# A two-layer hybrid decoder step on eight cores: unnormalised MLP input, conv and pool first, column chunks of w_in, time-major sample state

## The chip, the cores and the metric

The kernel runs on the eight cores of one Trainium2 chip. Each core takes one prompt sequence and four sample sequences; the cores exchange nothing. The metric is the device time in microseconds (us) of the slowest core. A program on eight cores has a second, slower state, in which the cores of one die show a lower granted TensorE clock; all comparisons below use runs of the fast state. Engines: PE multiplies matrices, DVE, ACT and POOL are the vector, scalar and general engines, SP only issues DMAs here. POOL and ACT can issue DMAs too.

## The reference, cut to what matters

```python
for layer in range(2):
    h = rmsnorm(x, norm1_g); proj = h @ w_in              # 1024 -> 2560
    u, q, k, v, gb, gc, gh = split(proj)
    y_pool = pool_mix(u)                                  # causal windows 2/4/8/16, 256 channels
    q, k = rope(rmsnorm(q)), rope(rmsnorm(k))
    y_attn = merge(dilated_attention(q, k, v))            # 3 groups: (128,1) (512,4) (2048,16)
    y_conv = gb * conv3(gc * gh)                          # 384 channels
    x = x + concat(y_pool, y_attn, y_conv) @ w_out        # 768 -> 1024
    x = x + square(relu(rmsnorm(x, norm2_g) @ w_up)) @ w_down   # 1024 -> 4096 -> 1024
# outputs also: the new sample caches, cache[:, 8:] followed by 8 new rows, for both layers
```

On each core x is 2080 tokens (32 sample, 2048 prompt), held as 5 blocks of 416 columns, with the 1024 channels as 8 chunks of 128 partitions. Moving the old cache rows into the output is a plain copy in HBM. Per layer and core it is four sequences times three caches of 120, 504 and 2040 KB (of 1024 bytes), 10.9 million bytes.

## The kernel before

The program is written as many small coroutines ("procs"). A planner in Python simulates the engines, decides from estimated costs and priorities in which order each engine gets its instructions, and derives the semaphore waits from reads and writes of named regions.

```python
def copy_caches(l, n, after):                 # HBM -> HBM, touches no buffer of SBUF
    yield wait(after)                         # planner event only
    for g in range(3):
        W = WINS[g]
        yield ops(ld(lambda e: e.dma_start(out=o_kv_s[g][l, n, 0:W - 8, :], in_=caches[g][l, n, 8:W, :]), 2000 * W, slot=("c2c", g)))
# ... placed after: att(l,0), att(l,1), and two points in the MLP

def reload(l, b, after):                      # x again, for the residual, into a slot that was scratch
    yield wait(*after)
    for h in range(2):
        yield ops(ld(...X[:, s, 4*h:4*h+4, :] <- xin or xpark...))     # ld = SP's queue
        for c in range(4 * h, 4 * h + 4):
            K.fire(ev("xres", l, b, c))

def norm(l, which, b, X, ..., on_pe=False):
    # sum of squares: on PE (layer 0's first norm, and one block of layer 1's) or by adds on POOL (all others)
    # rst = exp(-0.5 * ln(mean + eps)) on ACT
    # HT[c] = X[c] * g[c] * rst on DVE, 8 instructions, bf16: the input of w_in or w_up

def down(l, fb, b, oc):                       # MLP, quarter fb of the 4096
    # 8 matmuls, then X[oc] += psum on DVE
```

In the slots of x live, during a layer's front, the scratch of conv, pool, QKV and attention. So x is parked and loaded again ("reload") once a slot's scratch is dead, and out_proj's residual add (DVE, `X = psum + X`) waits for it.

## Time and profile before

| | before |
|---|---|
| time, median of 3 (range) | 1606.16 us (1603.94 to 1606.86) |
| PE, DVE, ACT, POOL busy, slowest core | 1424, 857, 479, 347 us of 1607 |
| layer 0 front / MLP / layer 1 front / MLP | 375 / 453 / 309 / 470 us |

The table of windows of the kernel before shows four stretches: per engine the busy time and (x) the instructions, then the granted PE clock, the DMA engines' busy share and GB/s.

```profile
core 7: us, PE busy (x) PEld busy (x) DVE busy (x) ACT busy (x) POOL busy (x), PEclk, DMA share, GB/s
0.00:375.00 375.00, 273.58 (x1755) 156.16 (x1756) 224.07 (x434) 151.22 (x362) 140.70 (x186) 0.90 0.67 126
375.00:828.00 453.00, 451.01 (x2563) 250.81 (x2562) 219.12 (x368) 110.50 (x217) 59.93 (x63) 1.00 0.30 61
828.00:1137.00 309.00, 240.64 (x1705) 140.92 (x1704) 202.24 (x398) 124.75 (x309) 123.77 (x154) 0.92 0.55 110
1137.00:1607.00 470.00, 459.02 (x2589) 253.92 (x2586) 211.99 (x349) 92.08 (x180) 23.01 (x24) 0.99 0.24 52
```

The two MLP stretches are PE work at full clock. The fronts have gaps, a lower clock, and DMA that is busy more than half the time. Who waited for whom on PE in the first 400 us of before (engine and line, what it waited for, total, times, longest):

```profile
PE psum L864 <- ACT sqr L863: 37.8, 16, 9.8
...
PE psum L1402 <- DVE big L1406: 9.9, 3, 5.7
```

L864 sums the squares of the norm on PE: those waits are mostly for x to arrive (ACT's squares, L863, waited 26.8 us for x in the first 120 us). L1402 is out_proj, held by the residual add L1406, which waits for the reload. Timeline of SP: start, duration, what; merged:

```profile
124.35 0.80 SPq L1462 DMA_DIRECT2D kv_s<-c  x1
...
288.55 0.58 SPq L916 DMA_DIRECT2D big<-xin  x1
...
315.58 11.48 SPq L916 DMA_DIRECT2D big<-xin  x8
327.11 3.65 SPq L1462 DMA_DIRECT2D kv_s<-c  x6
```

L916 is the reload, L1462 the cache copies. Two sequences' copies go out between 124 and 218 us; the other two go at 327 us.

### The profile page before, as it was taken

The page shows a single profiled execution, that of the slowest core. Times are in us where ns is not written, and L with a number is a line of the kernel's source. Part 1 is how long each engine was busy: PE and PEld are TensorE (multiplying, and loading weights), DVE is VectorE, ACT ScalarE, POOL GpSimd, SP SyncE. Part 2 cuts the span into 40 slices and gives each one's busy share as a digit, 9 for nine tenths or more (in the row PEclk, how much of TensorE's full clock was granted, in tenths as well). Part 3 has the DMA queues.
Part 4 walks back from the last instruction along what each step waited for, and adds up shares of the span by engine and source line. Part 5 has one row for each costly group of instructions (what it writes and reads, how often), then busy time and mean ns, then how long its engine had stood idle before and what let it go on. Part 6 is the DMA issues. An engine that isn't in the chain of part 4 may idle for free.

```text
span 1607.4 us, 26919 instructions; the slowest of 8 cores (1582.2 to 1607.4 us)
## 1 busy us (share of the span) xinstructions
PE 1424.3 (89%) x8606; PEld 801.8 (50%) x8606; DVE 857.4 (53%) x1547; ACT 478.5 (30%) x1065; POOL 347.4 (22%) x426
## 2 busy tenths in 40 slices
PE   2778788779999999999977789868699999999998
PEld 1344455434555555555544455534355555555554
DVE  1667667467444444445676666746854444444443
ACT  2544345424112212113433444532412111211211
POOL 2344344344000000012434344323500000000000
PEclk9789889899999999999999999989899999999999
DMA  8758541999223023033264452189920601400112
GB/s 184 167 75 71 111 111 34 137 234 171 49 49 58 1 53 53 1 63 76 86 148 57 68 133 74 36 127 241 169 50 1 105 1 28 79 1 1 44 69 102
DMA packets 67897, 133.32 MB, mean 83 GB/s; under 512 B 25832, under 2 KB 35112, under 8 KB 67376
## 3 DMA queue, kind: packets, MB, share of 16 engines
q0 software_dynamic: 27648, 54.14, 23.2%
q1 hardware_dynamic: 40112, 77.47, 18.1%
q8 instruction: 72, 1.18, 0.3%
q14 instruction: 65, 0.53, 0.2%
HBM read 159.71 MB, written 47.89 MB: 129 GB/s over the span
## 4 chain that ended last, share of the span: by engine, by line
PE 69%; DMA 10%; DVE 8%; issue 5%; POOL 4%; ACT 3%; SPq 1%; DVEq 0%; ACTq 0%; POOLq 0%
PE psum L1441 28%; PE psum L1425 27%; PE psum L923 5%; PE psum L1071 4%; DMA vspill<-big 4%; DMA big<-xin 3%; PE psum L1402 3%; DVE big L889 3%; DMA big<-w_in 2%; POOL sqr L875 1%; POOL big L1110 1%; POOL big L956 1%; DVE big L1118 1%; DVE big L1117 1%; DMA kv_p<-big 1%
## 5 line engine op out<-in xcount | busy, mean ns | idle before, releaser
L1425 PE MATMUL psum<-big 128*128 128x416 bf16 x2560 | 464.3, 341 | 4.3 <-DVE big L1406 2.2
L1441 PE MATMUL psum<-big 128*128 128x416 bf16 x2560 | 461.0, 339 | 1.5 <-DVE big L1431 1.5
L1430 ACT ACTIVATE big<-psum 128x416 f32<-128x416 f32 x320 | 165.1, 517 | 650.8 <-PE psum L1425 426.4
L1425 PEld LDWEIGHTS psum<-big 128*128 128x128 bf16 x2560 | 251.0, 98 | 206.8 <-issue 9.6
L1441 PEld LDWEIGHTS psum<-big 128*128 128x128 bf16 x2560 | 250.0, 98 | 201.5 <-issue 3.0
L1431 DVE TENSOR_TENSOR big<-psum,big 128x416 bf16<-128x416 f32 x320 | 187.9, 591 | 284.5 <-ACT big L1430 274.0
L1444 DVE TENSOR_TENSOR big<-psum,big 128x416 f32<-128x416 f32 x320 | 188.5, 591 | 200.4 <-PE psum L1441 199.7
L923 PE MATMUL psum<-big 128*128 128x416 bf16 x880 | 179.3, 355 | 10.6 <-ACT big L984 5.6
L1071 PE MATMUL psum<-big 128*128 128x384 bf16 (+1 forms) x816 | 156.5, 350 | 10.0 <-ACT big L1260 3.0
L889 DVE SCALAR_TENSOR_TENSOR big<-big 128x416 bf16<-128x416 f32 x160 | 120.7, 823 | 49.7 <-ACT big L886 42.6
L875 POOL TENSOR_TENSOR sqr<-sqr,big 128x416 fp32r<-128x416 f32 x98 | 107.9, 1101 | 172.1 <-ACT big L874 161.9
L923 PEld LDWEIGHTS psum<-big 128*128 128x128 bf16 x880 | 87.3, 102 | 80.5 <-issue 25.3
L1071 PEld LDWEIGHTS psum<-big 128*128 128x128 bf16 (+1 forms) x816 | 82.5, 104 | 73.9 <-issue 31.4
L1402 PE MATMUL psum<-big 128*128 128x416 bf16 x480 | 94.4, 356 | 15.4 <-DVE big L1406 13.2
L1110 POOL TENSOR_TENSOR big<-big 128x512 f32<-128x512 f32 (+1 forms) x54 | 66.7, 1238 | 184.2 <-DVE big L1104 170.2
L844 POOL DMA_DIRECT2D big<-w_up x16 | 12.2, 767 | 334.3 <-PE psum L1425 333.8
L874 ACT ACTIVATE big<-big 128x416 f32<-128x416 f32 x98 | 52.7, 547 | 98.4 <-DVE big L1406 62.5
L1402 PEld LDWEIGHTS psum<-big 128*128 128x128 bf16 x480 | 47.9, 102 | 58.3 <-issue 25.6
L956 POOL TENSOR_TENSOR big<-big 128x430 f32<-128x430 f32 (+7 forms) x72 | 64.7, 903 | 36.3 <-ACT big L952 28.4
L1406 DVE TENSOR_TENSOR big<-psum,big 128x416 f32<-128x416 f32 x80 | 45.3, 587 | 45.5 <-PE psum L1402 25.5
L864 PE MATMUL psum<-sqr,onesr 128*128 128x416 f32 x48 | 24.5, 567 | 40.3 <-ACT sqr L863 37.8
L1117 DVE TENSOR_TENSOR big<-big 128x128 f32<-128x128 f32 (+1 forms) x108 | 42.4, 393 | 27.7 <-POOL big L1110 21.8
(98 smaller groups left out, 892.9 us busy)
## 6 DMA issues: line engine op xcount, KB each, us to landing
big<-xin SPq DMA_DIRECT2D x20, 832.0 KB, 12.1
big<-w_up POOLq DMA_DIRECT2D x16, 1024.0 KB, 15.4
big<-w_down POOLq DMA_DIRECT2D x16, 1024.0 KB, 13.3
kv_s<-c SPq DMA_DIRECT2D x8, 2040.0 KB, 40.2
big<-w_in POOLq DMA_DIRECT2D x16, 576.0 KB, 8.7
xpark<-big SPq DMA_DIRECT2D x10, 832.0 KB, 3.6
big<-xpark SPq DMA_DIRECT2D x10, 832.0 KB, 15.7
yout<-big SPq DMA_DIRECT2D x20, 416.0 KB, 2.4
```

The costliest lines, as they stand in the source:

```text
L875: K.spawn(freeing(pool(BL, lambda e, i=i: e.tensor_tensor(out=acc, in0=acc.bitcast(F32), in1=SS[i], op=ALU.add), [ka, ("ss", i)], [ka]), P ...
L889: yield ops(*[dve(BL + 100, lambda e, c=c: e.scalar_tensor_tensor(out=HT[:, c, BL * b:BL * b + BL], in0=X[:, si, c, :], scalar=NG[:, l, wh ...
L923: yield ops(pe([(BL, lambda e, d=d: e.matmul(bank(bi)[:, 0:BL], lhsT=WA[:, d, col0:col0 + 128], rhs=HT[:, d, BL * b:BL * b + BL], start=(d ...
L956: return pool(n, lambda e: e.tensor_tensor(out=out, in0=a, in1=b_, op=ALU.add), r, w)
L1071: yield ops(pe([(384, lambda e, d=d, j=j, jj=jj: e.matmul(pq[0:R, jj, 0:384].rearrange("p (k n) -> p k n", k=3), lhsT=lhs(d, j), rhs=wg[:, ...
L1110: yield ops(pool(256 * J, lambda e: e.tensor_tensor(out=qf[0:R, 0:J, 0:256], in0=qf[0:R, 0:J, 0:256], in1=GQK[0:R].unsqueeze(1).to_broadca ...
L1402: yield ops(pe([(BL, lambda e, c=c: e.matmul(bank(bi)[:, 0:BL], lhsT=WO[c // 2][:, c % 2, 128 * oc:128 * oc + 128], rhs=mix(c, b), start=( ...
L1425: yield ops(pe([(BL, lambda e, d=d: e.matmul(bank(bi)[:, 0:BL], lhsT=WU[i][:, d, 128 * fc:128 * fc + 128], rhs=HT[:, d, BL * b:BL * b + BL ...
L1430: yield ops(act(BL, lambda e: e.activation(out=RL[ri], in_=bank(bi)[:, 0:BL], func=AF.Relu), [("ps", bi)], [("rl", ri)]))
L1431: yield ops(dve(BL, lambda e: e.tensor_tensor(out=AT[a][:, fc, :], in0=bank(bi)[:, 0:BL], in1=RL[ri], op=ALU.mult), [("ps", bi), ("rl", ri ...
L1441: yield ops(pe([(BL, lambda e, f=f: e.matmul(bank(bi)[:, 0:BL], lhsT=WD[i][:, f, 128 * oc:128 * oc + 128], rhs=AT[a][:, f, :], start=(f == ...
L1444: yield ops(dve(BL, lambda e: e.tensor_tensor(out=X[:, s, oc, :], in0=bank(bi)[:, 0:BL], in1=X[:, s, oc, :], op=ALU.add), [("ps", bi), ("x ...
```

## The change

In six parts:

1. The MLP takes x*g unnormalised. With v = mean(x^2) + eps, the squared ReLU makes the MLP's output scale by 1/v. So x is multiplied by v before the MLP's sums are added and the whole by 1/v at the end. Up-projections wait no longer for the norm.
2. Conv and pool get better priorities than attention.
3. w_in comes in column chunks (conv's c, h, b; pool; then q, k, v), x and weights in one order on POOL's queue.
4. The sample state is time-major: one transfer per kind instead of one per chunk.
5. Sums of squares are all on POOL (none on PE). The x reload goes from SP's queue to POOL's, the V spill from SP's to ACT's.
6. Cache copies are placed at four points in the MLP. Priorities and costs in the planner are retuned.

The core of the diff:

```diff
-    def norm(l, which, b, X, s, si, src, out_ev, before=(), on_pe=False):
+    def sumsq(l, which, b, X, s, si, src):          # POOL adds only, one buffer
...
+    def cast2(l, b, c):
+        yield wait(ev("xm", l, b, c))
+        yield ops(act(BL, ... out=HT[:, c, ...], in_=X[:, s, c, :], func=AF.Copy, scale=NG[:, l, 1, c:c + 1]))
+    def norm2(l, b):
+        bi = yield from sumsq(l, 1, b, ...)
+        yield ops(act(BL, ... out=VB[b], in_=bank(bi)[:, 0:BL], func=AF.Identity, scale=1.0 / D, bias=EPSC))
+        for c in range(8):
+            yield ops(dve(BL + 60, ... X[:, s, c, :] = X[:, s, c, :] * VB[b]))
+        yield ops(dve(BL + 60, ... e.reciprocal(out=VB[b], in_=VB[b])))
...
-    def reload(l, b, after):
-            yield ops(ld(lambda e: e.dma_start(out=X[:, s, 4 * h:4 * h + 4, :], in_=src[...
+    def reload(l, b, h, after):
+        yield ops(ldc(lambda e: e.dma_start(out=X[:, s, 4 * h:4 * h + 4, :], in_=src[...      # ldc = POOL's queue
...
     def down(l, fb, b, oc):
+        if fb == 0:
+            yield wait(ev("xv", l, b, oc))
         yield ops(dve(BL, ... X[oc] += psum))
+        if fb == 3:
+            yield ops(dve(BL + 60, ... X[oc] = X[oc] * VB[b]))
...
-                K.spawn(pool_item(l, b, pc), base + 120 + 40 * b)
+                K.spawn(pool_item(l, b, pc), base + 90 + 15 * b)
...
-        for n, e in enumerate((ev("att", l, 0), ev("att", l, 1), ev("um", l, 1, 2, 0), ev("um", l, 2, 2, 0))):
+        for n, e in enumerate((ev("um", l, 0, 4, 0), ev("um", l, 1, 1, 0), ev("um", l, 1, 4, 0), ev("um", l, 2, 2, 0))):
             K.spawn(copy_caches(l, n, e), base)
```

(`um` is an up-projection's matmuls: a point in the MLP.)

## The prediction

> **What bounds it now.** Four stretches (table of windows, slowest core): layer 0 before its MLP, 0–375 us: PE busy 274, granted clock 0.90, DMA share 0.67. MLP 0, 375–828: PE 451 of 453, clock 1.00. Layer 1 before its MLP, 828–1137: PE 241 of 309, clock 0.92. MLP 1, 1137–1607: PE 459 of 470. In the MLPs a matmul of 416 columns follows the last every 0.176 us, so those 923 us are PE work and stay. Only the 684 us outside can shrink. Estimated from the same spacing (in_proj 440, QKV 408, out_proj 240 matmuls a layer, plus attention) their PE work is about 235 us a layer, 470 in all: some 210 us of gaps and of cold clock. DVE there is busy 224 and 202 us, so it is a second floor close behind.
>
> Where the gaps are:
> - Start: to 40 us PE is busy 10 us; PE then waits 38 us in total for the squares of the norm (waits), which wait for x. Weights of conv land only at 102 us (chain: 10 us on w_in).
> - The chain has 16 and 24 us on the V spill (120–166 us): on the SP queue, behind other transfers; cache copies run then.
> - Layer end: 22.5 us on the reload of x (288–311), then chains of POOL adds of the norm (7 x 1.08 us a block), then Ln, Exp, and DVE multiplies of 0.82 us, before the first up-projection.
> - 828–900: norm at the boundary, then 5 us each on the small state load and stores, 10 us on kv_p.
>
> **What changes.**
> 1. The MLP no longer waits for norm 2: ACT casts x*g (about 0.55 us x 80) in place of DVE's 0.82 us x 80; POOL adds and Ln leave the chain. The price is DVE multiplies, 80 before and 80 after the MLP, about 0.65 us each (estimate), 104 us in all minus 66 removed. They lie in the MLP, where DVE is 45% busy; only in the last quarter of layer 0's MLP (0.59+0.59+0.65+0.82 us per 2.8 us of PE) does it get near full. Gain: 10–15 us a layer.
> 2. Conv and pool first, w_in by columns: with x0, x1 and one chunk loaded, PE starts useful work near 32–37 us and has done 60 us of it by about 105 us, against some 25 before. Gain 30–40 us.
> 3. Slots of conv and pool come free early, so x reloads early and out_proj of early blocks fills PE beside attention; cache copies move into the MLP, V spill to ACT's queue. Gain 25–35 us in layer 0, 20–30 in layer 1.
> 4. Layer 1: QKV doesn't wait for the last up-projection; state in one transfer per kind. Gain 10–20 us.
> 5. 48 fp32r matmuls of 0.43–0.57 us leave PE, 15–20 us of which perhaps 10 count; POOL takes 42 more adds of 1.1 us.
>
> Together these sum to more than I believe; attention without conv as filler will be bound by DVE/ACT/POOL latency and takes some back. I expect layer 0's front about 320 us, layer 1's about 275, MLPs 925 with small losses at the seams.
>
> **Prediction: 1520 us, 80% range 1470 to 1565. Faster by over 2%: 0.90; within 2%: 0.08; slower: 0.02.**
>
> **What would show it.** Saturated PE at about 310–325 us (375 before); L1 front 260–290 us; no Ln/Exp between out_proj and up; MLP stretches at 0.176 us a matmul; PE clock nearer 1 outside the MLP; no 20 us V-spill or reload pieces in the chain.
>
> **What would make it wrong.** All loads on POOL's queue behind POOL's adds; QKV starting late because wq is loaded after x3; attention's latency left bare at the end of the front; DVE full in the last quarter of layer 0's MLP, so that PE waits for PSUM banks.

## More of the kernel before

**An event such as `ev("att", l, 0)` lives in the planner alone.** It decides when an instruction is placed in its engine's list. On the chip, the instruction waits only for semaphores of data that it reads or overwrites.

## The result, and the profile after

| | before | after |
|---|---|---|
| time, median of 3 | 1606.16 us | 1667.07 us (1666.92, 1667.07 and one slow run of 1794.89) |
| ratio of fast runs | 1 | 1.0382, 95% interval 1.0352 to 1.0412 |
| PE / DVE / ACT / POOL busy | 1424 / 857 / 479 / 347 | 1416 / 939 / 519 / 412 |

Ratios are the mean time of one kernel's fast runs over that of the other's of the same rounds, so not quite the ratio of the medians quoted; a median is over all runs, the slow ones included. The change is 3.8% slower. The forecast was 5% faster.

To see where the time went, I counted matmuls done by a given time, from one window a count, from 0, restricted to one line of the kernel (a few records can be missing from a trace). Multiplying by the measured spacing, 0.176 us for 416 columns and 0.163 us for QKV, gives the useful PE work done:

| matmuls done by | before: in_proj / QKV / out_proj / up + down | after | after leads by |
|---|---|---|---|
| 160 us | 144 / 216 / 0 / 0 | 387 / 88 / 0 / 0 | 22 us, less some 4 us of attention |
| 320 us | 433 / 408 / 48 / 0 | 440 / 408 / 96 / 26 | 14 us |
| 440 us | 440 / 408 / 240 / 353 | 440 / 408 / 240 / 196 | -28 us |

The change was ahead until 320 us, and lost 42 us in the next 120. The table of windows around that place, before and then after:

```profile
320.00:360.00 40.00, 29.67 (x156) 15.29 (x153) 28.26 (x45) 10.65 (x21) 15.93 (x17) 0.94 1.03 235
360.00:400.00 40.00, 34.48 (x177) 18.04 (x178) 26.43 (x39) 18.59 (x38) 18.90 (x18) 0.91 0.98 172
400.00:440.00 40.00, 40.00 (x229) 22.24 (x228) 20.67 (x37) 5.69 (x11) 0.00 (x0) 1.00 0.32 56
```

```profile
320.00:360.00 40.00, 11.43 (x74) 6.08 (x71) 9.24 (x9) 6.55 (x12) 11.12 (x13) 0.63 1.01 187
360.00:400.00 40.00, 17.17 (x68) 8.01 (x69) 10.75 (x20) 9.68 (x19) 5.63 (x6) 0.71 0.98 205
400.00:440.00 40.00, 38.41 (x211) 20.77 (x210) 35.48 (x49) 22.28 (x43) 20.00 (x20) 0.97 0.71 132
```

After, PE is busy 29 of 80 us, at a clock of 0.63 and 0.71, and DVE idles with it. DMA is at its full share in both kernels. The stall costs more than its length: 24 matmuls of out_proj that came right after a wait of 13.4 us took 7.00 us (383.30), where 24 others took 4.38 (365.56). The Trainium skill, "TensorE: Matmul & The Clock Gate", section "What's actually happening", says that idle time halves PE's clock and activity restores it; a mean of 0.63 with long gaps and 1.00 in the MLP agree. PE's waits and the DVE add that they end on (waits of DVE, 300 to 430 us, then of PE, 0 to 430 us, both of after):

```profile
DVE big L1452 <- DMA big<-xin: 49.0, 3, 20.7
```

```profile
PE psum L1448 <- DVE big L1452: 38.3, 4, 15.8
PE psum L877 <- POOL sqr L873: 22.7, 1, 22.7
PE psum L1024 <- DVE big L1018: 14.7, 2, 9.4
```

out_proj (L1448) waits for the residual add (L1452), which waits for the reload of x. Layer 1 has the same pair of waits (PE 43.1 us, DVE 49.4). The second and third lines are a slow start, to which we come later. When were the reload and the copies issued? SP's timeline of after (L1514 is the copies, L1516 a small copy that goes with them), then POOL's (L936 is the reload, L848 the MLP weights):

```profile
315.96 1.83 SPq L1514 DMA_DIRECT2D kv_s<-c  x3
317.83 0.65 SPq L1516 DMA_DIRECT2D pool_old<-spool_rows  x1
318.52 6.44 SPq L1514 DMA_DIRECT2D kv_s<-c  x9
```

```profile
302.27 1.58 POOL L848 DMA_DIRECT2D big<-w_down  x2
...
325.42 1.16 POOL L936 DMA_DIRECT2D big<-xin  x2 [15.23 <-DMA kv_p<-big]
...
335.63 2.14 POOL L936 DMA_DIRECT2D big<-xin  x4
```

All twelve copies of the layer went out between 316 and 325 us, in the front, not in the MLP. The last three blocks' reload followed from 325 us, on another queue, into DMA engines that had 10.9 MB of copies to do. The DMA issues of the page (KB each, median us from issue to landing) show what that did to the reload of layer 1 (before, then after):

```profile
big<-xpark SPq DMA_DIRECT2D x10, 832.0 KB, 15.7
```

```profile
big<-xpark POOLq DMA_DIRECT2D x10, 832.0 KB, 45.1
```

The reload moved in one step from SP's list, where it had been standing ahead of the copies, to POOL's. That left SP's list short, with nothing in front of the copies to hold them. They were placed later in the plan, and started earlier on the chip. The Trainium skill says in "DMA: Bandwidth & Descriptors", section "Issuing engines are not separate DMA queues", that DMAs from the scalar, sync or gpsimd engine "will ultimately run on the same 16 DMA engines and interleave with each other": the 45.1 us above, on a queue that held no copies, agree.

Theory A is then: the copies, released early, cost the time. Two rivals stood beside it. B: the reload itself is badly placed on POOL, whose list stalls 15.2 us for a kv_p store ahead of it (this wait ends at 325.42 above) and whose queue has w_down before it. C: the multiplies of the unnormalised MLP load DVE. Its busy time rose by 81 us.

### The profile page after: what moved, and what is told of

Its sections match the earlier page's. It is cut to its first block, busy times and chain, and to the rows that moved or that the text cites. A ratio compares the mean times of both kernels' runs of the same rounds, so it can differ in the third digit from the quotient of the medians.

```text
span 1665.3 us, 27077 instructions; the slowest of 8 cores (1650.9 to 1665.3 us)
## 1 busy us (share of the span) xinstructions
PE 1415.6 (85%) x8564; PEld 793.8 (48%) x8564; DVE 938.7 (56%) x1637; ACT 519.0 (31%) x1135; POOL 412.5 (25%) x489
## 4 chain that ended last, share of the span: by engine, by line
PE 66%; DMA 9%; DVE 9%; issue 5%; POOL 3%; another core or an unknown queue 3%; ACT 2%; SPq 0%; DVEq 0%; ACTq 0%; POOLq 0%
PE psum L1488 26%; PE psum L1471 25%; PE psum L944 5%; PE psum L1111 5%; PE psum L1448 3%; DVE big L890 3%; DMA vspill<-big 3%; DMA big<-xpark 2%; DMA big<-xin 2%; DMA kv_p<-big 2%; POOL sqr L873 1%; POOL big L1150 1%; DVE big L1157 1%; DMA big<-vspill 1%
## 5 line engine op out<-in xcount | busy, mean ns | idle before, releaser
L1478 DVE TENSOR_TENSOR big<-psum,big 128x416 bf16<-128x416 f32 x320 | 187.4, 588 | 256.7 <-ACT big L1477 255.1
L873 POOL TENSOR_TENSOR sqr<-sqr,big 128x416 fp32r<-128x416 f32 x140 | 162.4, 1160 | 206.3 <-ACT big L872 187.2
L1448 PE MATMUL psum<-big 128*128 128x416 bf16 x480 | 103.3, 376 | 87.9 <-DVE big L1452 81.4
L1448 PEld LDWEIGHTS psum<-big 128*128 128x128 bf16 x480 | 50.0, 106 | 134.8 <-issue 106.9
L1452 DVE TENSOR_TENSOR big<-psum,big 128x416 f32<-128x416 f32 x80 | 45.9, 587 | 116.7 <-DMA big<-xpark 49.4
L872 ACT ACTIVATE big<-big 128x416 f32<-128x416 f32 x140 | 74.2, 545 | 71.8 <-POOL sqr L873 34.8
L899 ACT ACTIVATE big<-big 128x416 bf16<-128x416 f32 x80 | 50.3, 638 | 123.5 <-DVE big L1452 122.7
L848 POOL DMA_DIRECT2D big<-w_up x16 | 12.3, 769 | 298.9 <-PE psum L1471 298.7
L890 DVE SCALAR_TENSOR_TENSOR big<-big 128x416 bf16<-128x416 f32 x80 | 65.3, 884 | 25.9 <-ACT big L887 25.9
L998 POOL TENSOR_TENSOR big<-big 128x430 f32<-128x430 f32 (+8 forms) x72 | 65.8, 919 | 40.5 <-ACT big L994 31.4
L910 DVE TENSOR_TENSOR big<-big 128x416 f32<-128x416 f32 x80 | 61.5, 793 | 3.5 <-ACT big L906 3.3
## 6 DMA issues: line engine op xcount, KB each, us to landing
big<-xpark POOLq DMA_DIRECT2D x10, 832.0 KB, 45.1
```

What stands on the lines that cost most here:

```text
L872: yield ops(act(BL, lambda e: e.activation(out=SS[i], in_=X[:, si, c, :], func=AF.Square), [("x", s, c)], [("ss", i)]))
L873: K.spawn(freeing(pool(BL, lambda e, i=i: e.tensor_tensor(out=acc, in0=acc.bitcast(F32), in1=SS[i], op=ALU.add), ["sqr", ("ss", i)], ["sqr"]),
L890: yield ops(*[dve(BL + 200, lambda e, c=c: e.scalar_tensor_tensor(out=HT[:, c, BL * b:BL * b + BL], in0=X[:, si, c, :], scalar=NG[:, l, 0, ...
L1448: yield ops(pe([(BL, lambda e, c=c: e.matmul(bank(bi)[:, 0:BL], lhsT=WO[c // 2][:, c % 2, 128 * oc:128 * oc + 128], rhs=mix(c, b), start=( ...
L1478: yield ops(dve(BL, lambda e: e.tensor_tensor(out=AT[a][:, fc, :], in0=bank(bi)[:, 0:BL], in1=RL[ri], op=ALU.mult), [("ps", bi), ("rl", ri ...
```

## The experiments

Ten kernels ran, one of them twice, in three sets on three chips. Each set had its own runs of the kernel before. Ratios are to those. Unless said otherwise the results were correct.

| set | kernel | median us | ratio to before (95%) |
|---|---|---|---|
| 1 | after, copies held back | 1573.78 | 0.9813 (0.9746 to 0.9880) |
| 1 | after, no copies (wrong) | 1579.83 | 0.9844 (0.9770 to 0.9918) |
| 1 | after, copies held back, reload on SP | 1551.48 | 0.9683 (0.9621 to 0.9744) |
| 1 | before, copies held back | 1601.89 | 0.9988 (0.9921 to 1.0055) |
| 2 | after, reload on SP only | 1560.64 | 0.9777 (0.9753 to 0.9801) |
| 2 | before, copies put ahead of the reload | 1710.03 | 1.0708 (1.0681 to 1.0736) |
| 2 | held back, reload on SP, normalised MLP | 1548.98 | 0.9724 (0.9673 to 0.9776) |
| 2 | held back, reload on SP, first norm on PE | 1523.1 and 1523.4 (the two fast runs of four) | 0.9542 (0.9512 to 0.9571) |
| 3 | the same again | 1503.64 | 0.9442 (0.9420 to 0.9465) |
| 3 | the same, normalised MLP | 1508.14 | 0.9470 (0.9448 to 0.9493) |
| 3 | the same, old priorities | 1533.96 | 0.9635 (0.9608 to 0.9663) |

One kernel, the fastest, ran in sets 2 and 3: 0.954 and 0.944, with intervals that don't touch. So about 1% between sets is not the kernel (the chip is the likely reason), and smaller differences are read only within a set.

One caution for all that follows. An edit makes the planner run again, and the planner may then choose another order for every engine. In experiments 1 and 2 PE's order of instructions is that of after, as the traces show. In the others it is not: in experiments 3 and 5 it differs from about the 1500th of 8564 matmuls on. Those runs measure the edit together with its new order.

### 1. Holding the copies back

The wait is on a constant value of PE's semaphore. The order of the instructions on every engine stays as it was.

```diff
+    def ld_after_pe(fn, nbytes, slot):
+        def emit():
+            o = S.dma(fn, slot=slot)
+            d = S.ops["pe"][-1]          # the PE instruction that the planner placed last
+            d.signal = True
+            o.waits.append(d)
+            return [o]
+        return ("sp", 0.06, emit, [(0.0, [], [])], nbytes)
...
-            yield ops(ld(lambda e: e.dma_start(out=o_kv_s[g]...
+            yield ops(ld_after_pe(lambda e: e.dma_start(out=o_kv_s[g]...
```

> The kernel after, with one thing added: each copy of a cache waits on the chip for the PE instruction that the planner had issued last when it placed the copy (a constant semaphore value), so the copies can start only inside the MLP. Order of all instructions unchanged. Theory A (copies): in the kernel after the 12 copies of a layer, 10.6 MB, start at 316 to 325 us and 1124 to 1133 us, in front of the x reload of the last three blocks, which then lands 35 to 62 us after issue; held back, the reload lands within 30 us, 30 to 45 us a layer come back, and the time is 1580 to 1605 us. Theory B (the reload sits on POOL's queue behind w_down and behind POOL's wait for a kv_p store) and theory C (the extra DVE multiplies of the unnormalised MLP): little changes, 1645 us or more.

Measured: 1573.78 us, 0.9813 against 1.0382 of the unmended change. By 440 us, up plus down had 422 matmuls done, 196 in after. SP's timeline now has the copies in the MLP, and the reload of layer 1 lands in 7.2 us instead of 45.1:

```profile
449.05 8.94 SPq L1523 DMA_DIRECT2D kv_s<-c  x3
```

```profile
big<-xpark POOLq DMA_DIRECT2D x10, 832.0 KB, 7.2
```

The gain, 93 us between the medians of two chips (0.057 of before's 1605 us is 91), is even a little more than theory A had expected (it said 1580 to 1605). It turns the change from a loss into a gain of 1.9%. C is out as the cause of the loss: all its multiplies are still there.

### 2. Leaving the copies out

```diff
-            yield ops(ld(lambda e: e.dma_start(out=o_kv_s[g]...
+            pass
```

> The kernel after without the 24 cache copies (wrong result on purpose: those output rows stay unwritten). Theory A: the whole cost of the copies goes, 1575 to 1600 us, within 10 us of the run with held-back copies, and the reload lands within 30 us. Theories B and C: 1640 us or more.

Measured: 1579.83 us, 0.9844, within the interval of the first. Results are wrong (rows of three outputs unwritten). Copies that are held back to the MLP cost no time that these runs can show. That they move 22 MB in the two layers is no matter there: it is the place that counts.

### 3. The reload back on SP's queue

```diff
-        yield ops(ldc(lambda e: e.dma_start(out=X[:, s, 4 * h:4 * h + 4, :], in_=src[...
+        yield ops(ld(lambda e: e.dma_start(out=X[:, s, 4 * h:4 * h + 4, :], in_=src[...
```

> Copies held back as in the first run of this set, and the x reload issued from the SP queue instead of POOL's. Against that first run: theory B expects 15 us or more less a layer (POOL no longer stands 15 us at the wait for the kv_p store, and the reload does not queue behind w_down); theory A alone expects less than 10 us of difference in all.

Measured: 1551.48 us, 22 us less than with the copies held back alone, in the same set. That lies between the two: theory B had said 15 us or more a layer, 30 in all, and theory A less than 10. So the edit is worth 22 us, but B's reason for it is not shown, and the traces speak against it as the whole. In the first run POOL stood at the reload for kv_p for 8.4 to 12.2 us in layer 0, by core, and for 0.7 to 3.6 us in layer 1. The gain lies the other way round: the median core starts the last matmul of layer 0's MLP 5 us earlier (802.7 us against 807.7), and gains another 12 us in layer 1. Nor is it V: PE's waits for V on its way back through HBM (19.3 us on the profiled core of the first run) end, the two long ones, at 193 and 990 us, each before POOL's stall at the reload of its layer, and other cores of this run still have up to 15.0 us of them. The new order that the planner made is a rival that stands untested.

It is not plainly a faster queue either. With the copies held back, the reload's median landing was 7.2 us from SP and 7.5 from POOL in layer 0, and 11.8 and 7.2 in layer 1, where SP issued six of the ten within 5.3 us. The Trainium skill's sentence that issue from sync or scalar "is generally faster" ("DMA: Bandwidth & Descriptors", section "Issuing engine by pattern") is neither borne out nor refuted by these 832 KB transfers.

### 4. Control: the copies of before, held back

> Control: the kernel before, with the copies moved to the same events in the MLP and held back there by the same wait. Theory A: before had half of the copies between 124 and 218 us, beside V spills that took 16 and 24 us of the chain, and half behind the reload at 327 us, so it gains less than the kernel after: 5 to 25 us a layer, 1560 to 1597 us. If the copies are nothing special (B, C), it stays within 1% of 1606 us.

Its edit is the wait of experiment 1 and the four events of the change, in the kernel before. Measured: 1601.89 us, 0.9988. A miss for theory A's numbers (it had said 5 to 25 us a layer): before lost nothing to its copies that this run can show. The copies are not bad wherever they lie in a front; ahead of something that PE waits for they are.

### 5. Only the reload on SP, copies not held back

> The kernel after with the x reload issued from SP's queue, without the wait on the copies. SP takes its instructions in order, and in the program the reloads stand ahead of the copies, which so again start behind the reload, as in the kernel before. Theory A (it is the order of copies and reload that cost 93 us): within 15 us of the run with both edits (1551 us), so 1550 to 1570 us. If the copies hurt wherever they fall near the end of the front, they now meet the first MLP weights and the time is 1590 us or more.

Measured: 1560.64 us, 0.9777. As theory A expected: SP's list has the reloads ahead of the copies again, and copies start at 327 us behind them, as its timeline shows (L936 is the reload, L1514 the copies):

```profile
309.62 17.57 SPq L936 DMA_DIRECT2D big<-xin  x4
327.24 2.58 SPq L1514 DMA_DIRECT2D kv_s<-c  x3
```

One word of the change, the queue of the reload, with the order that the planner makes from it, decided some 6%. To hold the copies back as well adds about 1% (0.9683 in the other set), about what two chips can differ by; whether that last step is real is open.

### 6. The reverse, in the kernel before

```diff
-        for n, e in enumerate((ev("att", l, 0), ev("att", l, 1), ev("um", l, 1, 2, 0), ev("um", l, 2, 2, 0))):
+        for n, e in enumerate((*[ev("att", l, 2)] * 4,)):
```

> Reverse test: the kernel before, with all four copies of a layer placed after the attention of block 2, so that SP issues them ahead of the x reload. Theory A: 10.6 MB ahead of the reload cost what they cost in the kernel after, less what before already loses there, 20 to 45 us a layer: 1645 to 1695 us. If the loss needs something else of the change (reload on POOL's queue, the new norm), before stays under 1625 us.

Measured: 1710.03 us, 1.0708: 112 us lost, more than expected. The waits of PE between 240 and 480 us say on what:

```profile
PE psum L1273 <- DMA big<-vspill: 62.7, 1, 62.7
PE psum L1402 <- DVE big L1406: 4.4, 2, 2.4
```

It is not the reload but V's way back from HBM for attention that was stuck behind the copies, 62.7 us here and 50.9 us in layer 1. So this is no exact mirror of the change. What the two kernels have in common: 10.9 MB of copies ahead of a transfer that PE needs at the end of a front (the reload in after, V here) cost 46 to 56 us a layer.

### 7. What the unnormalised MLP is worth

The edit puts Ln, Exp and the DVE multiply by g and the scale back into `norm2`, and drops `cast2` and the multiplies of x. It ran twice, on two versions:

> Copies held back and reload on SP (1551 us), with the normalised MLP put back: Ln, Exp, and a DVE multiply by g and the scale into the MLP's input; no cast on ACT, no multiplies of x. The prediction's step 1 (10 to 15 us a layer): 1570 to 1582 us. If the extra DVE work of the unnormalised MLP (61 + 54 + 27 us against 66) eats the gain: 1545 to 1556 us or less.

> The same with the normalised MLP put back. The last pair of runs showed a difference of less than 0.5%, within its interval. The prediction's 10 to 15 us a layer would be 1.3 to 2% more than the fastest version; a washed-out gain is within 0.6% of it either way.

Measured: 1548.98 us (0.9724; its counterpart had 0.9683, in the other set), and, side by side in five rounds, 1508.14 us against 1503.64: 0.9470 against 0.9442. The rewriting is worth 4.5 us, 0.3%. The prediction gave it 20 to 30. Its price was also higher than estimated. The groups of DVE instructions of after (busy us, mean ns of one, idle time before them and what ended it), first multiplies, last multiplies, reciprocal:

```profile
L910 DVE TENSOR_TENSOR big<-big 128x416 f32<-128x416 f32 x80 | 61.5, 793 | 3.5 <-ACT big L906 3.3
L1497 DVE TENSOR_TENSOR big<-big 128x416 f32<-128x416 f32 x80 | 53.9, 680 | 5.5
...
L912 DVE RECIPROCAL big<-big 128x416 f32<-128x416 f32 x10 | 27.4, 2742 | 0.3
```

That is 143 us in all, where the prediction had 104. The reciprocal was not in the prediction at all: a median of 2740 ns where the multiplies of that shape have 592. The Trainium skill, "VectorE: DVE Perf Modes", section "First, the fixed hardware budget", describes reciprocal as an iterative divide with a repeat count of 8. That may be the reason; no run here tests it, and the page gives no time. Single multiplies take from 578 to 1916 ns (L910). "SBUF — State Buffer", section "SBUF: two separate sides", says that a DVE instruction with two SBUF inputs and a POOL instruction that reads SBUF exclude each other for their whole length. These multiplies have two SBUF inputs, and after's trace agrees: of the 160 of both lines, the 95 with no POOL compute instruction beside them took 572 to 594 ns, and all 48 that took more than 600 ns had one beside them. From 420.4 to 424.1 us, beside POOL's adds, L910 took 0.95 us a piece, while L1478, a DVE multiply with one input in PSUM, took 0.58. I estimate that this is some 21 of the 143 us (115.4 us less 160 times 0.592).

Why so little gain? Because PE no longer lacks work where the norm used to hold it: with the reload early, out_proj of other blocks and the first up-projections lie beside it. With the normalised MLP (second version), PE is busy 117 of the 120 us from 280 to 400, and 114 with the unnormalised. That is the reason the two traces offer; it is argued, not tried. What the rewriting is worth where the reload is late was not tried either.

### 8. The sums of layer 0's first norm, back on PE

```diff
+    SQR2 = es.enter_context(nc.sbuf_tensor("sqr2", [128, BL], F32R))
-    SS = [M([128, BL], F32, ("ss", i)) for i in range(3)]
+    SS = [M([128, BL], F32, ("ss", i)) for i in range(2)]
...
     def sumsq(l, which, b, X, s, si, src):
+        if l == 0 and which == 0:
+            # (code left out: ACT squares chunk c into one of two fp32r buffers, PE adds it up with a matmul by ones)
```

> Copies held back and reload on SP (1551 us), with the sums of squares of layer 0's first norm back on PE, as in the kernel before (two fp32r buffers; one buffer of the later norms given up for the room). If POOL (busy 28.5 of the first 40 us, and PE's 22.7 us wait for its adds) is what keeps the start slow: 5 to 12 us less. If loads and DVE set the start, within 3 us of 1551.

Measured: 0.9542 against 0.9724 in the same set (that one has also the normalised MLP, worth 0.3%): by ratio 29 us and by median 26, so 20 to 25 us less for this edit, twice what was expected. (The edit also takes one of three buffers from the later norms.) The table of windows of the version without this edit (reload on SP, copies held back), and then with it:

```profile
0.00:20.00 20.00, 0.00 (x0) 0.00 (x0) 0.06 (x1) 5.35 (x9) 18.08 (x29) 1.00 0.85 212
20.00:40.00 20.00, 9.36 (x24) 3.33 (x25) 9.43 (x8) 7.03 (x14) 10.47 (x12) 1.00 1.17 167
40.00:60.00 20.00, 16.29 (x92) 8.66 (x90) 18.06 (x35) 8.82 (x22) 12.88 (x17) 1.00 1.15 230
60.00:80.00 20.00, 8.16 (x34) 3.78 (x34) 16.04 (x20) 6.87 (x14) 16.36 (x21) 0.66 1.03 194
```

```profile
0.00:20.00 20.00, 6.65 (x12) 3.36 (x12) 2.12 (x5) 8.54 (x16) 12.91 (x26) 1.00 0.89 218
20.00:40.00 20.00, 17.53 (x72) 8.50 (x73) 12.59 (x28) 6.82 (x14) 2.64 (x6) 0.99 1.17 174
40.00:60.00 20.00, 19.64 (x98) 10.57 (x96) 13.08 (x28) 11.01 (x24) 6.94 (x12) 0.87 1.15 223
60.00:80.00 20.00, 17.86 (x98) 9.51 (x97) 18.96 (x32) 9.35 (x19) 13.10 (x20) 1.00 1.00 194
```

POOL was busy 18 of the first 20 us, with issuing DMAs and clearing buffers and then with seven adds of 1.1 us a block. PE's first matmul came at 22.7 us; its waits for the pool mixer (L1024 in after: 14.7 us) stood behind POOL's adds as well, since that mixer's sums are POOL's too; with the edit they fall to 3.1 us. With the edit, in_proj has 238 matmuls done by 80 us, against 144. The work that the change had taken off PE was done there while PE had nothing else to do.

> The fastest version again (copies held back, reload on SP, layer 0's first norm summed on PE), in five rounds and beside the next two. If the 1523 us of its fast runs hold: 0.950 to 0.958 of the kernel before.

The repetition: 1503.64 us, ratio 0.9442. The expected 0.950 to 0.958 is missed on the good side (another chip). It is the fastest version, 9.1% faster than the change as made by the ratio of 0.9442 to 1.0382, and correct.

### 9. The old priorities of conv and pool

```diff
-                K.spawn(pool_item(l, b, pc), base + 90 + 15 * b)
+                K.spawn(pool_item(l, b, pc), base + 120 + 40 * b)
-                K.spawn(conv_item(l, b, cc), base + 91 + 15 * b + cc)
+                K.spawn(conv_item(l, b, cc), base + 121 + 40 * b + cc)
```

> The fastest version with the planner's priorities of conv and pool as in the kernel before (behind the attention blocks instead of ahead); loads and slots as in the change. If conv and pool ahead of attention are worth something by themselves (early reload, out_proj as filler): 10 to 30 us more. If the order is set by the loads and slots anyway: within 5 us.

Measured: 1533.96 us, 0.9635 against 0.9442 in the same set: 30 us more. So this part of the change was right and is worth 30 us. Nothing of it is in layer 0: there out_proj and MLP stand no later at 440 us (240 / 753 matmuls with the old priorities, 240 / 731 with the change's), since loads and slots set the order. It is all in layer 1. SP's timeline there, with the change's priorities and then with the old ones (L959 is the reload):

```profile
1023.55 5.56 SPq L959 DMA_DIRECT2D big<-xpark  x6
```

```profile
972.80 0.99 SPq L959 DMA_DIRECT2D big<-xpark  x2
...
994.68 13.79 SPq L959 DMA_DIRECT2D big<-xpark  x8
```

With conv and pool late, their slots come free late, and eight of ten reloads go out in one burst at 995 us, with PE busy 23.5 of the 40 us from 980 (33.3 with the change's priorities). With conv and pool first, four had gone before.

## Why the prediction was wrong

- **What bounds the kernel**: right. The MLPs stayed at 0.176 us a matmul in all runs, and all the loss and all the gain was in the fronts.
- **"cache copies move into the MLP"** (step 3): this is the step that failed. They moved into the MLP in the planner's list alone; on the chip all twelve went out in the front, at 316 to 325 us in layer 0. I read the events as waits. A look at what the copies wait for on the chip (nothing), and at what stood ahead of them on SP's queue in before (the reload, at 315.58 us) would have shown that taking the reload off SP sets the copies free. Against a forecast gain of 45 to 65 us from the whole of step 3, the early copies cost 91 to 93 us (experiment 1).
- **"x reloads early", out_proj as filler** (step 3): right in kind. At 320 us the change had 96 matmuls of out_proj done, 48 in before. But only the reload of the first two blocks was early; the last three wait for the end of QKV or of attention in both kernels.
- **Conv and pool first** (step 2): mechanism right, held back by step 5. By 105 us the change had done matmuls of in_proj and QKV worth 40 us, before 22: 18 us gained, not 30 to 40. With the start mended (experiment 8), the fastest version has done 62 us by then, as the prediction said (60). By 120 us it has 368 matmuls of in_proj and 58 of QKV, against 56 and 136 in before.
- **48 matmuls leave PE, "perhaps 10" us gained** (step 5): wrong in sign. PE had idle time for them where they were, and the 40 that experiment 8 put back had cost 20 to 25 us on POOL. "All loads on POOL's queue behind POOL's adds" stood among the things that could make the prediction wrong, and part of it did.
- **Unnormalised MLP, 10 to 15 us a layer** (step 1): mechanism right, size wrong: 4.5 us in both layers, at 143 us of DVE where I had 104.
- **Layer 1's state in one transfer, QKV not waiting** (step 4): not tried alone; open.
- **V spill on ACT's queue**: not tried alone. After's chain still has pieces of 17.2, 10.1 and 15.6 us on the spill (before: 16.3, 23.6 and 18.5), and two of 35 us on the reload, where the prediction expected no 20 us pieces of either.
- **The size**: with the two slips mended, by undoing most of part 5 and adding a wait, what is left of the change is worth 5.6% (0.9442). I had forecast 1520 from 1606, 5.4%. That the two agree is in part luck: step 1 gave 4.5 us for the 20 to 30 forecast, and steps 3 and 4 were not measured one by one.

## What to carry to other kernels

An order in a planner, or in source text, is not a wait: a DMA without a data dependence starts when its queue gets to it, so moving another transfer off that queue can release it early (here, at 316 us, in the front). Before moving a DMA to another queue, list what stands behind it and what it was holding back; and give bulk copies with no reader an explicit wait for the stage that has DMA to spare. Work is cheapest on the engine that idles at that moment: sums taken off a busy-on-average PE were put on the one engine that was full in that stage.

## What the Trainium skill lacked or had wrong

- "VectorE: DVE Perf Modes" gives reciprocal's repeat count but no time: on 128x416 fp32 it took 2740 ns (ten of ten between 2734 and 2753), 4.6 times the 592 ns of a multiply.
- "DMA: Bandwidth & Descriptors" calls issue from sync or scalar generally faster, without setting the two beside each other for a large load: with no copies beside it, the 832 KB reload landed (median) in 7.2 us from SP and 7.5 from POOL in layer 0, and in 11.8 and 7.2 in layer 1. What the choice of queue decided here is what starts early behind it (12 copies a layer, 91 to 93 us).
- No page that I read gives a number for what a bulk HBM-to-HBM copy does to loads that run beside it: the reload's median landing went from 7.2 to 45.1 us with 10.9 MB of copies issued just before.
